# Gate matmuls of a gated recurrence: full-height block-diagonal weights, or pairs of 64-row blocks in the two halves of the array

## The chip, the cores and the metric

The kernel runs on one core of a Trainium2 chip. The metric is device time in microseconds (us) of one launch. Besides the launches that were only timed there is one execution with a hardware profile, and all rows shown come from such profiles. In them PE is the matmul engine (TensorE), PEld its weight loads, DVE is VectorE, ACT is ScalarE, POOL is GpSimd, SP is SyncE, and a q behind a name means that engine's queue of instructions that only issue transfers or wait.

## The reference

One layer of a decoder block, 2048 positions by 1024 features, in float32. One input projection feeds two branches. Branch A is banded, dilated attention. Branch B is a width-4 convolution and a gated linear recurrence (RG-LRU). Both are gated, projected, merged, projected again and normalised. The part that matters here is the two gates of the recurrence, r and i: each is a matmul with a block-diagonal matrix of 16 blocks of 64 by 64.

```python
proj = x @ w_in + b_in
q, k, v, g_attn, u_lru, g_lru, gate_logits = split(proj)
...                                             # branch A: attention
u = causal_depthwise_conv(u_lru, conv_w, conv_b)
xb = u.reshape(B, S, 16, 64)
r = sigmoid(einsum('bsgi,gij->bsgj', xb, w_r).reshape(B, S, C) + b_r)
i = sigmoid(einsum('bsgi,gij->bsgj', xb, w_i).reshape(B, S, C) + b_i)
log_a = -8.0 * r * softplus(-lam)
a, mult = exp(log_a), sqrt(max(-expm1(2.0 * log_a), 0))
h = associative_scan(h[t] = a[t] * h[t-1] + mult[t] * i[t] * u[t])
...
out = (sigmoid(gA) * y_a + sigmoid(gB) * y_b) @ w_out + b_out
return layer_norm(alpha * x + out)
```

## The kernel before

Everything is feature-major: 128 features on the partitions, positions along the free axis in chunks of 512 (`CH`). A float32 product is made of three matmuls in the type fp32r: both factors are split into a rounded high part and a remainder, and high times high, high times low and low times high are added up in one PSUM bank.

The program has three stages. The first is the input projection, from the start to about 1480 us. It is cut into steps (`plan`), each a pair of 128-feature columns for two chunks of positions; a step has seven products (a Strassen-like scheme) of twelve 128x128x512 matmuls. One product is one tick of the loop over `where`. The matmuls of a product all stand on line 598 (`product`), whatever the tiles; their results land in one of four PSUM banks `q` and are taken out by `evacuate`. Around the products runs everything that hangs on the projection's results: rotary embedding, stores, the gates of the branches and the whole recurrence. Each of these is a generator (a chain) that asks at every yield for free slots and for a share of an engine's time (`Ask`); `run_chains` lets it go on in some tick when both are there. The order of each engine's queue is the order in which this Python code emits, and nothing moves it later. The second stage is the attention (about 1480 to 1830 us), the third the output projections and the normalisation.

The recurrence is the chain `lru(i, c, ub)`: 8 groups `i` of 128 features (two 64-blocks each) by 4 chunks `c` of positions, 32 in all, at most two alive at a time. In it, in this order:

- SP fetches the gate weights `gr` (lines 434 and 435): the host has laid out `wr[i]` and `wi[i]` as 128x128 matrices, two 64x64 blocks on the diagonal and zeros beside them. This happens 16 times, twice for each group. ACT (line 452) and DVE split them into high and low, `gw`.
- The convolution's result `v` is split into `vh` and `vl`.
- `gates` hands PE six matmuls, lines 468 to 470, three for r into one PSUM bank `g`, three for i into the other. They are put in by `pe_later`, which means after the sixth matmul of a product of the next tick.
- ACT reads the two banks with a tanh each (lines 481 and 482, into `tr` and `ti`; the sigmoid's half and shift are folded in later), then runs three more operations on `tr`, lines 483 to 485. DVE waits for `ti` on line 486.
- The rest, to the scan on line 503, is DVE and ACT work on 128x512 tiles.

Of the kernel before, what the change touches and what calls it, by code (L numbers as in the profile page):

```python
# [8 lines left out]
F32 = mybir.dt.float32  # L9
F32R = mybir.dt.float32r  # L10
AF = mybir.ActivationFunctionType
ALU = mybir.AluOpType
# [3 lines left out]
P = 128  # L16
# [4 lines left out]
CH = 512  # L21
# [10 lines left out]
def hybrid_block_kernel(ctx: ExitStack, tc: tile.TileContext, a: dict, out: bass.AP):  # L32
    nc = tc.nc
    sp, act, dve, pool, pe = nc.sync, nc.scalar, nc.vector, nc.gpsimd, nc.tensor

    def flat(t):
        return t.bitcast(F32)
# [37 lines left out]
    lr = cst.tile([P, 8, 8], F32, name="lr")  # L75
    act.dma_start(lr, a["lru_vec"])
    brh = cst.tile([P, 2, 8], F32, name="brh")
    sp2 = cst.tile([P, 8], F32, name="sp2")


    X = ctx.enter_context(tc.tile_pool(name="X", bufs=1))
# [11 lines left out]
    def pe_later(lag, fn):  # L93
        pe_late.append((now["n"] + lag, fn))
# [27 lines left out]
    ps = stA.enter_context(tc.tile_pool(name="ps", bufs=2, space=PSUM))  # L122
# [5 lines left out]
    def take(name, dt=F32R):  # L128
        if not vacant:
            raise RuntimeError(f"no slot at {now['n']}: {[x[1].name if hasattr(x[1],'name') else x[1] for x in home.values()]} chains {len(chains)}")  # L130
        i = vacant.pop(0)
        t = sl_p.tile([P, CH], dt, tag=f"s{i}", name=name)
        home[id(t)] = (i, t)
        return t

    def give(*ts):
        for t in ts:
            vacant.append(home.pop(id(t))[0])

    def give_sent(*ts):  # L140

        for t in ts:
            later(2, lambda t=t: give(t))
# [69 lines left out]
    def tt(eng, out, in0, in1, op):  # L213
        eng.tensor_tensor(out=out, in0=in0, in1=in1, op=op)  # L214
# [202 lines left out]
    GLG, GW = {}, {}  # L417
# [5 lines left out]
    def lru(i, c, ub):  # L423
        nm = f"{i}_{c}"
        f = FT_U + i
        if c == 1 and i in put_off:
            yield Ask(lag=0, need=1, keep=1, cond=lambda: len(ub_free) > 1)
            ub = ub_free.pop(0)
            sp.dma_start(ub[:, 3:3 + CH], u_scr[i])
        bring_gw = c in ((0, 1) if i in put_off else (0, 2))  # L430
        if bring_gw:
            yield Ask(lag=0, need=1, keep=1)
            gr = take("gr" + nm, F32)
            sp.dma_start(gr[:, 0:P], a["wr"][i])
            sp.dma_start(gr[:, P:2 * P], a["wi"][i])
        if c == 1 and i in put_off:
            yield Ask(lag=4)
        yield Ask(lag=0, need=1, keep=6, cond=lambda: gate["live"] < 2 and begun[i] == c, ACT=1.3, DVE=2.7)
        gate["live"] += 1
        begun[i] += 1  # L440
        v = take("v" + nm, F32)
        act.activation(ub[:, 0:3], ubs[:, i, c, 0:3], AF.Copy)
        act.activation(v, ub[:, 0:CH], AF.Identity, scale=lrn[:, 0, i:i + 1], bias=lr[:, 4, i:i + 1])
        for j in range(1, 4):
            dve.scalar_tensor_tensor(out=v, in0=ub[:, j:j + CH], scalar=lrn[:, j, i:i + 1], in1=v,
                                     op0=ALU.mult, op1=ALU.add)
        act.activation(ubs[:, i, c + 1, 0:3], ub[:, CH:CH + 3], AF.Copy)
        ub_free.append(ub)
        if bring_gw:
            yield Ask(ACT=.4, DVE=.4, lag=2, need=1, keep=1)  # L450
            w = GW[i] = take("gw" + nm)
            act.activation(w[:, 0:2 * P], gr[:, 0:2 * P], AF.Copy)
            tt(dve, w[:, 2 * P:], gr[:, 0:2 * P], flat(w[:, 0:2 * P]), ALU.subtract)
            give(gr)
        yield Ask(lag=0, cond=lambda: gated[i] == c)
        gw = GW[i].rearrange("p (l j f) -> p l j f", l=2, j=2)
        yield Ask(need=2, keep=1, ACT=.66, DVE=.75)
        vh, vl = take("vh" + nm), take("vl" + nm)
        act.activation(vh, v, AF.Copy)
        tt(dve, vl, v, flat(vh), ALU.subtract)  # L460
        yield Ask(lag=2, cond=lambda: not gate["busy"])
        gate["busy"] = True
        pg = []

        def gates():
            for j in range(2):
                g = ps.tile([P, CH], F32, tag="g", name=f"g{j}{nm}", bufs=2)
                pe.matmul(g, gw[:, 0, j], vh, start=True, stop=False)
                pe.matmul(g, gw[:, 0, j], vl, start=False, stop=False)
                pe.matmul(g, gw[:, 1, j], vh, start=False, stop=True)  # L470
                pg.append(g)
            give(vh, vl)
            if c in ((0, 3) if i in put_off else (1, 3)):
                give(GW[i])

        pe_later(1, gates)
        gated[i] = c + 1
        yield Ask(lag=2, need=3, keep=1, ACT=3.3, DVE=.75)
        gate["busy"] = False
        tr, ti, e = take("tr" + nm, F32), take("ti" + nm, F32), take("e" + nm, F32)  # L480
        act.activation(tr, pg[0], AF.Tanh, scale=0.5, bias=brh[:, 0, i:i + 1])
        act.activation(ti, pg[1], AF.Tanh, scale=0.5, bias=brh[:, 1, i:i + 1])
        act.activation(e, tr, AF.Exp, scale=sp2n[:, i:i + 1], bias=sp2n[:, i:i + 1])
        act.activation(e, e, AF.Identity, scale=0.5, bias=half_t)
        act.activation(tr, tr, AF.Tanh, scale=sp2[:, i:i + 1], bias=sp2[:, i:i + 1])
        dve.scalar_tensor_tensor(out=ti, in0=ti, scalar=1.0, in1=v, op0=ALU.add, op1=ALU.mult)
        give(v)
        yield Ask(need=2, keep=1, ACT=2.0, DVE=2.2)
        s, w = take("sq" + nm, F32), take("nw" + nm, F32)
        act.activation(s, tr, AF.Sqrt)  # L490

        dve.scalar_tensor_tensor(out=w, in0=tr, scalar=1.0, in1=e, op0=ALU.add, op1=ALU.mult)
        dve.scalar_tensor_tensor(out=e, in0=w, scalar=2.0, in1=e, op0=ALU.subtract, op1=ALU.mult)
        dve.scalar_tensor_tensor(out=tr, in0=tr, scalar=2.0, in1=e, op0=ALU.mult, op1=ALU.mult)
        give(w)
        yield Ask(ACT=.66, DVE=1.5)
        act.activation(tr, tr, AF.Identity, bias=one_t)
        dve.scalar_tensor_tensor(out=s, in0=s, scalar=-1.0, in1=e, op0=ALU.mult, op1=ALU.mult)
        tt(dve, s, s, ti, ALU.mult)
        give(e, ti)  # L500
        yield Ask(need=1, keep=1, DVE=1.6, cond=lambda: done[i] == c)
        h = take("h" + nm, F32)
        dve.tensor_tensor_scan(out=h, data0=tr, data1=s, initial=hst[:, i, 0:1], op0=ALU.mult, op1=ALU.add)
        dve.tensor_copy(hst[:, i, 0:1], h[:, CH - 1:CH])
        done[i] = c + 1
        gate["live"] -= 1
        give(tr, s)
        if c == 1 and i in put_off:
            yield Ask(lag=0, need=1, keep=3)
            g = GLG[i, 1] = take("glg" + nm, F32)  # L510
            sp.dma_start(g, hb_scr[i * P:(i + 1) * P, CH:2 * CH])
            yield Ask(lag=2)
        yield Ask(POOL=1.4, cond=lambda: (i, c) in GLG)
        g = GLG.pop((i, c))
        tt(pool, g, g, h, ALU.mult)
        give(h)
        yield Ask()
        sp.dma_start(hb_scr[i * P:(i + 1) * P, c * CH:(c + 1) * CH], g)
        give_sent(g)
# [160 lines left out]
    for s, pl in enumerate(plan):  # L680
        if pl[0] and pl[4] == "ug":
            i = pl[1][1][0] - FT_U
            if i not in put_off:
                continue
            at(base[s] - 12, lambda i=i: start_chain(lru(i, 1, None)))
# [168 lines left out]
    def consts():  # L854
        dve.tensor_scalar(out=bh, in0=b72, scalar1=0.5, scalar2=None, op0=ALU.mult)
        dve.tensor_scalar(out=bn, in0=b72, scalar1=-1.0, scalar2=None, op0=ALU.mult)
        dve.tensor_scalar(out=brh, in0=lr[:, 5:7, :], scalar1=0.5, scalar2=None, op0=ALU.mult)
        dve.tensor_scalar(out=lrn, in0=lr[:, 0:4, :], scalar1=-1.0, scalar2=None, op0=ALU.mult)
        dve.memset(ubs, 0.0)
        dve.memset(hst, 0.0)  # L860
# [20 lines left out]
    at(0, lambda: prep_w(0, 1))  # L881
    at(0, lambda: [one_block("B21", kk) for kk in K4])
    at(0, consts)
    at(1, lambda: prep_w(0, 2))
    at(1, lambda: [one_block("B12", kk) for kk in K4])
# [37 lines left out]
    n = len(where)  # L923
# [137 lines left out]
    for m in range(NB + 4):  # L1061
        u, n = divmod(m, 16)
# [156 lines left out]
    for n in range(32):  # L1219
        c, f = divmod(n, 8)  # L1220
# [211 lines left out]
```

## Time and profile before

| | |
|---|---|
| time, three runs | 2267.12, 2267.64, 2272.91 us; median 2267.64 |
| span of the profiled execution, first to last instruction | 2268.7 us |
| PE busy | 2213.9 us (98%), 11032 matmuls |
| PEld busy | 1868.7 us (82%) |
| DVE, ACT, POOL busy | 1752.4 (77%), 1091.3 (48%), 874.6 us (39%) |
| mean granted TensorE clock | 0.991 |

The page gives the profiled execution's span and no other time of it; the median of the timed runs lies 1.1 us below that span. The busy time of PE counts each matmul to its modelled end, and one matmul begins while the one before is still in flight, so PE's real pace is read from the distance between the starts of neighbouring matmuls and not from the mean duration of a matmul.

### The profile page before, as it was taken

Reading aid. Unit: us, or ns where it says so; the run is one execution under the profiler, and the core shown is the slowest. Engines: PE = TensorE matmul, PEld = TensorE weight load, DVE = VectorE, ACT = ScalarE, POOL = GpSimd, SP = SyncE. Lnnn points to the kernel's source line nnn. Section 1 sums busy time; section 2 is a strip of 40 time slices with the busy share of each in tenths; the row PEclk is TensorE's granted clock in tenths of the full one; section 3 lists DMA queues with packets and bytes.
Section 4 is the critical chain, followed back from the end, with each engine's and each line's share of the span. In section 5 each row is a group of like instructions: output and inputs, shape, how many; then the busy total and the mean of one; then the engine's idle time right before and its main releaser. Section 6 shows DMA issues by size and latency. Waiting matters only on the chain.

```text
span 2268.7 us, 34220 instructions
## 1 busy us (share of the span) xinstructions
PE 2213.9 (98%) x11032; PEld 1868.7 (82%) x11032; DVE 1752.4 (77%) x3234; ACT 1091.3 (48%) x1982; POOL 874.6 (39%) x640
## 2 busy tenths in 40 slices
PE   7999999999999999999999999989999999999998
PEld 6888878888787788888888888878999888788887
DVE  8788878999898877778778878655666668967777
ACT  5344545456455656556566566555666621121010
POOL 1545544555454022222222212257676426722220
PEclk9999999999999999999999999999999999999999
DMA  7998897988987777686888787897786679884441
GB/s 227 268 259 254 244 266 222 273 267 269 273 266 249 258 215 225 201 241 208 252 276 258 249 250 237 251 256 176 206 217 160 191 234 316 287 271 167 130 140 65
DMA packets 327954, 526.01 MB, mean 232 GB/s; under 512 B 97120, under 2 KB 138080, under 8 KB 322912
## 3 DMA queue, kind: packets, MB, share of 16 engines
q1 hardware_dynamic: 297008, 479.05, 68.1%
q0 software_dynamic: 10080, 18.35, 5.1%
q10 hardware_dynamic: 20688, 26.42, 3.7%
q8 instruction: 88, 1.44, 0.3%
q14 instruction: 90, 0.74, 0.1%
HBM read 318.38 MB, written 190.64 MB: 224 GB/s over the span
## 4 chain that ended last, share of the span: by engine, by line
PE 57%; DMA 6%; DVE 2%; ACT 1%; POOL 1%; issue 1%; SPq 1%; ACTq 0%; DVEq 0%; POOLq 0%
PE q L598 29%; PE o L1012 4%; PE s L973 3%; PE z L1304 2%; PE z L1305 2%; PE z L1303 2%; PE yb L1198 2%; PE yb L1200 2%; PE yb L1199 2%; PE pt L988 2%; DMA A<-qh_scr 2%; PE ya L1271 1%; PE ya L1272 1%; PE ya L1270 1%; DMA l<-wl_scr 1%
## 5 line engine op out<-in xcount | busy, mean ns | idle before, releaser
L598 PE MATMUL q<-xT,hS 128*128 128x512 f32 x1680 | 520.9, 391 | 7.2 <-ACT e L621 6.0
L598 PE MATMUL q<-xT,l 128*128 128x512 f32 x1120 | 437.1, 390 | 0.0
L598 PE MATMUL q<-xB,hA 128*128 128x512 f32 x1248 | 389.7, 394 | 10.1 <-ACT xB L202 5.7
L598 PEld LDWEIGHTS q<-xT,hS 128*128 128x128 f32 x1680 | 314.9, 188 | 73.0 <-ACT e L621 6.4
L598 PE MATMUL q<-xB,l 128*128 128x512 f32 x904 | 354.6, 392 | 1.4 <-DMA l<-wl_scr 1.3
L598 PEld LDWEIGHTS q<-xB,hA 128*128 128x128 f32 x1248 | 234.7, 189 | 61.0 <-ACT xB L202 5.7
L598 PEld LDWEIGHTS q<-xT,l 128*128 128x128 f32 x1120 | 210.7, 188 | 44.1
L979 ACT ACTIVATE p<-p,osb 128x256 f32<-128x256 f32 (+1 forms) x384 | 156.2, 454 | 118.4 <-DVE osb L977 117.7
L214 POOL TENSOR_TENSOR S<-S,wA 128x512 f32<-128x512 f32 x35 | 45.7, 1306 | 422.6 <-DVE S L214 251.7
L977 DVE CUSTOM_DVE_ANT_0 p<-s,mask 128x256 f32<-128x256 f32 (+1 forms) x384 | 125.2, 364 | 103.0 <-PE s L973 61.5
L598 PEld LDWEIGHTS q<-xB,l 128*128 128x128 f32 x904 | 171.0, 189 | 38.5 <-DMA l<-wl_scr 2.2
L214 POOL TENSOR_TENSOR sw<-sw,sin 128x512 f32<-128x512 f32 x96 | 161.8, 1691 | 70.3 <-DMA sw<-y 64.6
L259 ACT ACTIVATE hA<-wA 128x512 fp32r<-128x512 f32 x218 | 135.5, 624 | 89.6 <-DMA wA<-in_w_in_dram 52.7
L598 PE MATMUL q<-xB,hS 128*128 128x512 f32 x560 | 174.9, 394 | 3.0 <-DVE v L214 3.0
L598 PE MATMUL q<-xT,hA 128*128 128x512 f32 x560 | 173.1, 390 | 3.1 <-ACT hi L323 1.8
L1012 PE MATMUL o<-V,ptb 128*128 128x65 f32 x1200 | 166.4, 277 | 8.0 <-ACT ptb L993 5.3
L1012 PEld LDWEIGHTS o<-V,ptb 128*128 128x128 f32 x1200 | 153.3, 196 | 19.4 <-ACT ptb L993 16.2
L259 ACT ACTIVATE hS<-S 128x512 fp32r<-128x512 f32 x175 | 109.2, 624 | 97.1 <-DVE S L214 51.3
L214 POOL TENSOR_TENSOR l<-wA,hA 128x512 fp32r<-128x512 f32 x68 | 105.2, 1547 | 80.3 <-ACT hA L259 61.6
L973 PE MATMUL s<-B,A 128*128 128x256 f32 (+1 forms) x384 | 116.8, 326 | 10.0 <-DMA A<-qh_scr 6.4
L598 PEld LDWEIGHTS q<-xT,hA 128*128 128x128 f32 x560 | 104.6, 188 | 26.6 <-issue 3.7
L598 PEld LDWEIGHTS q<-xB,hS 128*128 128x128 f32 x560 | 104.7, 189 | 25.1 <-issue 4.1
(196 smaller groups left out, 4853.0 us busy)
## 6 DMA issues: line engine op xcount, KB each, us to landing
wA<-in_w_in_dram SPq DMA_DIRECT2D x253, 256.0 KB, 5.0
wl_scr<-l SPq DMA_DIRECT2D x105, 512.0 KB, 5.3
l<-wl_scr SPq DMA_DIRECT2D x105, 512.0 KB, 4.7
sw<-y SPq DMA_DIRECT2D x384, 64.0 KB, 3.3
wS<-in_w_in_dram SPq DMA_DIRECT2D x70, 256.0 KB, 4.7
wS<-in_w_in_dram POOLq DMA_DIRECT2D x70, 256.0 KB, 6.6
o_scr<-osb ACTq DMA_DIRECT2D x48, 264.0 KB, 5.9
oc<-o_scr SPq DMA_DIRECT2D x48, 264.0 KB, 5.0
```

The costliest lines, as they stand in the source:

```text
L214: eng.tensor_tensor(out=out, in0=in0, in1=in1, op=op)
L259: act.activation(h, r, AF.Copy)
L598: pe.matmul(bank, w[:, ks], x[:, kk, xx], start=(first and i == 0), stop=(last and i == 11))
L973: pe.matmul(s[:, h, (0 if g == 2 and n else lo):256], q, k, start=(i == 0), stop=(i == 1))
L977: dve.tensor_tensor_reduce(out=p[:, h, lo:256], in0=s[:, h, lo:256], in1=mask[:, lo:256], scale=1.0, scalar=3e38, op0=ALU.add, op1=ALU.min ...
L979: act.activation(p[:, h, lo:256], p[:, h, lo:256], AF.Exp, scale=-1.0, bias=mm)
L988: pe.transpose(pt[:, 2 * h + x, :], p[:, h, x * P:(x + 1) * P], ident)
L1012: pe.matmul(o[:, n % 2, h * 65:h * 65 + 65], ptb[:, 2 * h + x, :], V[:, kb, vo + h * 65:vo + h * 65 + 65], start=(x == lo // P), stop=(x = ...
L1198: pe.matmul(yb, WL[f][:, 0, k], xx[:, 0], start=(k == 0), stop=False)
L1199: pe.matmul(yb, WL[f][:, 0, k], xx[:, 1], start=False, stop=False)
L1200: pe.matmul(yb, WL[f][:, 1, k], xx[:, 0], start=False, stop=(k == 7))
L1303: pe.matmul(z, mh[:, k], w[:, 0, hs], start=(k == 0), stop=False)
```

## The change

The diagonal matrices of 128 rows go. A group's two 64-feature blocks are each kept in their own half of the partitions, as a 64x128 matrix: in the lower half (partitions 0 to 63) block 2i with its r weights in columns 0 to 63 and its i weights in columns 64 to 127; in the upper half block 2i+1 with i first and r second. A gate evaluation is then three pairs of matmuls of 64 rows: in each pair one matmul works on the rows 0 to 63 and writes bank `g0`, the other on the rows 64 to 127 and writes bank `g1`. In the built program these matmuls carry a tile of 64x128, at row 0 and at row 64, where all others have 128x128. The number of matmuls stays at six for each gate evaluation.

Each bank now holds r of one block in one half of its partitions and i of the same block in the other. So the two tanh of 128 partitions become four of 64, and two of them write another half than they read. The biases `brh` are gathered to match by four small transfers on ACT's queue at the start of the program. The weights are fetched by four transfers of 64x64 where two of 128x128 were, and the two operations that split them work on 128x128 where they worked on 128x256.

```diff
+    HALF = (slice(0, 64), slice(64, P))
+    for hs, os in (HALF, HALF[::-1]):
+        act.dma_start(brh[hs, 0], a["lru_vec"][hs, 5])
+        act.dma_start(brh[hs, 1], a["lru_vec"][os, 6])
...
             gr = take("gr" + nm, F32)
-            sp.dma_start(gr[:, 0:P], a["wr"][i])
-            sp.dma_start(gr[:, P:2 * P], a["wi"][i])
+            for hs, n in ((HALF[0], ("wr", "wi")), (HALF[1], ("wi", "wr"))):
+                for j in range(2):
+                    sp.dma_start(gr[hs, HALF[j]], a[n[j]][i, hs, hs])
...
-            act.activation(w[:, 0:2 * P], gr[:, 0:2 * P], AF.Copy)
-            tt(dve, w[:, 2 * P:], gr[:, 0:2 * P], flat(w[:, 0:2 * P]), ALU.subtract)
+            act.activation(w[:, 0:P], gr[:, 0:P], AF.Copy)
+            tt(dve, w[:, P:2 * P], gr[:, 0:P], flat(w[:, 0:P]), ALU.subtract)
...
-        gw = GW[i].rearrange("p (l j f) -> p l j f", l=2, j=2)
+        gw = GW[i].rearrange("p (l f) -> p l f", f=P)
...
         def gates():
-            for j in range(2):
-                g = ps.tile([P, CH], F32, tag="g", name=f"g{j}{nm}", bufs=2)
-                pe.matmul(g, gw[:, 0, j], vh, start=True, stop=False)
-                pe.matmul(g, gw[:, 0, j], vl, start=False, stop=False)
-                pe.matmul(g, gw[:, 1, j], vh, start=False, stop=True)
-                pg.append(g)
+            pg[:] = [ps.tile([P, CH], F32, tag="g", name=f"g{j}{nm}", bufs=2) for j in range(2)]
+            for k, (l, x) in enumerate(((0, vh), (0, vl), (1, vh))):
+                for hs, g in zip(HALF, pg):
+                    pe.matmul(g, gw[hs, l], x[hs], start=(k == 0), stop=(k == 2))
...
-        act.activation(tr, pg[0], AF.Tanh, scale=0.5, bias=brh[:, 0, i:i + 1])
-        act.activation(ti, pg[1], AF.Tanh, scale=0.5, bias=brh[:, 1, i:i + 1])
+        for h, (hs, os) in enumerate((HALF, HALF[::-1])):
+            act.activation(tr[hs], pg[h][hs], AF.Tanh, scale=0.5, bias=brh[hs, 0, i:i + 1])
+            act.activation(ti[hs], pg[h][os], AF.Tanh, scale=0.5, bias=brh[os, 1, i:i + 1])
...
-        dve.tensor_scalar(out=brh, in0=lr[:, 5:7, :], scalar1=0.5, scalar2=None, op0=ALU.mult)
+        dve.tensor_scalar(out=brh, in0=brh, scalar1=0.5, scalar2=None, op0=ALU.mult)
```

On PE, this is the first gate evaluation in the program, group 0 and chunk 0, in the middle of a product `q0` of step 6. `g00` and `g10` are the two banks, `vh0` and `vl0` the parts of the convolved input, `gw0` the weights. Before:

```order
L598 MATMUL q0_6_1450<-xB11_272,l0_6_1349 128x512
L468 MATMUL g00_0_1457<-vh0_0_1379,gw0_0_1352 128x512
L469 MATMUL g00_0_1457<-vl0_0_1380,gw0_0_1352 128x512
L470 MATMUL g00_0_1457<-vh0_0_1379,gw0_0_1352 128x512
L468 MATMUL g10_0_1461<-vh0_0_1379,gw0_0_1352 128x512
L469 MATMUL g10_0_1461<-vl0_0_1380,gw0_0_1352 128x512
L470 MATMUL g10_0_1461<-vh0_0_1379,gw0_0_1352 128x512
L598 MATMUL q0_6_1450<-xB11_272,hA11_6_1347 128x512 x2
```

And the same place in the changed program, whose line numbers are 4 to 6 higher:

```order
L602 MATMUL q0_6_1456<-xB11_276,l0_6_1355 128x512
L474 MATMUL g00_0_1463<-vh0_0_1385,gw0_0_1358 128x512
L474 MATMUL g10_0_1464<-vh0_0_1385,gw0_0_1358 128x512
L474 MATMUL g00_0_1463<-vl0_0_1386,gw0_0_1358 128x512
L474 MATMUL g10_0_1464<-vl0_0_1386,gw0_0_1358 128x512
L474 MATMUL g00_0_1463<-vh0_0_1385,gw0_0_1358 128x512
L474 MATMUL g10_0_1464<-vh0_0_1385,gw0_0_1358 128x512
L602 MATMUL q0_6_1456<-xB11_276,hA11_6_1353 128x512 x2
```

The six stand at the same place between the matmuls of the projection. They now alternate between the two banks, and so between the two halves of the array, where they filled one bank after the other.

On ACT, the same gate evaluation a little later, from the evacuation before it to the three operations on `tr0` behind it. Before:

```order
L259 ACTIVATE hA22_6_1502<-wA22_6_1257 128x512
L481 ACTIVATE tr0_0_1506<-g00_0_1457,brh_198 128x512
L482 ACTIVATE ti0_0_1507<-g10_0_1461,brh_198 128x512
L483 ACTIVATE e0_0_1508<-tr0_0_1506,sp2n_227 128x512
L484 ACTIVATE e0_0_1508<-e0_0_1508,half_t_211 128x512
L485 ACTIVATE tr0_0_1506<-tr0_0_1506,sp2_199 128x512
L259 ACTIVATE hS4_6_1531<-S4_6_1318 128x512
```

After:

```order
L263 ACTIVATE hA22_6_1508<-wA22_6_1263 128x512
L485 ACTIVATE tr0_0_1512<-g00_0_1463,brh_198 64x512
L486 ACTIVATE ti0_0_1513<-g00_0_1463,brh_198 64x512
L485 ACTIVATE tr0_0_1512<-g10_0_1464,brh_198 64x512
L486 ACTIVATE ti0_0_1513<-g10_0_1464,brh_198 64x512
L487 ACTIVATE e0_0_1514<-tr0_0_1512,sp2n_231 128x512
L488 ACTIVATE e0_0_1514<-e0_0_1514,half_t_215 128x512
L489 ACTIVATE tr0_0_1512<-tr0_0_1512,sp2_199 128x512
L263 ACTIVATE hS4_6_1539<-S4_6_1324 128x512
```

Two operations more stand ahead of everything that follows on ACT, and `ti0` is whole only after the fourth. Apart from these places, the two more transfers for each fetch of weights and the four at the start, the order on every engine is as before.

## The prediction

> **What bounds the kernel now.** I read the stages first. The view by windows gives the busy time of each engine in stretches of the projection stage, which ends near 1480 us and holds all 32 gate evaluations. The first column is the stretch and its length; a number after x is a count of instructions.
>
> ```profile
> core 0: us, PE busy (x) PEld busy (x) DVE busy (x) ACT busy (x) POOL busy (x), PEclk, DMA share, GB/s
> 200.00:400.00 200.00, 194.92 (x879) 159.52 (x878) 169.01 (x203) 100.79 (x165) 100.74 (x75) 0.99 0.86 248
> 400.00:600.00 200.00, 199.16 (x878) 164.26 (x877) 185.70 (x216) 101.98 (x170) 110.00 (x81) 1.00 0.90 266
> 600.00:800.00 200.00, 194.31 (x844) 158.77 (x843) 169.51 (x222) 112.88 (x188) 67.84 (x52) 0.99 0.84 265
> 800.00:1000.00 200.00, 200.00 (x907) 165.66 (x906) 153.12 (x210) 111.44 (x181) 45.81 (x31) 1.00 0.74 218
> 1200.00:1481.00 281.00, 279.67 (x1234) 231.25 (x1232) 222.89 (x298) 172.08 (x270) 72.60 (x50) 1.00 0.80 250
> ```
>
> PE is the bound: it is busy all 200 us from 800 to 1000 us. Before 800 us DVE stands close behind (185.70 of 200 us from 400 to 600), after it there is room (153.12). ACT is at most about 61% busy (172.08 of 281 us). So a microsecond taken from PE is a microsecond won in the later part, and perhaps less in the earlier, where PE also waits a few times. A delay on ACT or DVE costs something only where it reaches PE.
>
> Next, the timeline of PE at the first gate evaluation: start, length, line, tiles.
>
> ```profile
> 137.04 0.39 PE L598 MATMUL q<-xB,l 128*128 128x512 f32 x1
> 137.27 0.39 PE L468 MATMUL g<-vh,gw 128*128 128x512 f32 x1
> 137.50 0.39 PE L469 MATMUL g<-vl,gw 128*128 128x512 f32 x1
> 137.72 0.39 PE L470 MATMUL g<-vh,gw 128*128 128x512 f32 x1
> 137.95 0.39 PE L468 MATMUL g<-vh,gw 128*128 128x512 f32 x1
> 138.18 0.39 PE L469 MATMUL g<-vl,gw 128*128 128x512 f32 x1
> 138.40 0.39 PE L470 MATMUL g<-vh,gw 128*128 128x512 f32 x1
> 138.63 0.62 PE L598 MATMUL q<-xB,hA 128*128 128x512 f32 x2
> ```
>
> Each matmul lasts 0.39 us, but one starts every 0.227 us. The six occupy PE from 137.27 to 138.63, 1.36 us, and the projection goes on without a gap on either side. Thirty-two times 1.36 is 43.5 us: all that the gates cost PE now, of which perfect pairing could take half, 21.8 us or 1.0%.
>
> **The change part by part.**
>
> *Pairs.* If the two halves of a pair run side by side, three pairs need 3 x 0.227 = 0.68 us. No row of this trace has a 64-row matmul, so this is bounded: 0.68 us below, and 6 x 0.227 = 1.36 us if the halves go one after the other. I take the low end, because the two work on different rows of the array and write different banks, and nothing that one needs is made by the other.
>
> The weights could still set the pace, since six loads remain for three pairs. The attention's short matmuls show how fast loads can go. Here eight matmuls of 65 columns stand in one row, and the next row begins when they are through:
>
> ```profile
> 1600.60 1.00 PE L1012 MATMUL o<-V,ptb 128*128 128x65 f32 x8
> 1601.41 0.31 PE L973 MATMUL s<-B,A 128*128 128x128 f32 x1
> ```
>
> From 1600.60 to 1601.41 is 0.81 us, 0.10 us for each load with its matmul. Two loads, 0.20 us, fit under the 0.227 us of a pair. Only the second load of the first pair stands alone: 0.10 us more.
>
> *Whether loads may run ahead.* This is the load of the first gate matmul, on PEld:
>
> ```profile
> 137.05 0.19 PEld L468 LDWEIGHTS g<-vh,gw 128*128 128x128 f32 x1
> ```
>
> It lies inside the projection's matmul of 137.04, which uses the same 128 rows. The Trainium skill (TensorE: Matmul & The Clock Gate, Part 3: Packing small matmuls) says that a load overlaps a matmul in flight only where their row groups differ; this trace does not agree. By that rule the second and third pair would each have to wait for their loads, and the sum below would lose about 0.4 us for each gate evaluation. I keep to the row.
>
> *Two switches.* PE goes from 128-row to 64-row tiles and back around every gate evaluation. Nothing in this trace shows such a switch. At the least it costs nothing. The nearest row for the other end is a restart of PE from empty, when a matmul cannot begin until the one before has left the array and its weights come in uncovered:
>
> ```profile
> 313.65 0.39 PE L598 MATMUL q<-xB,l 128*128 128x512 f32 x1
> 315.79 0.70 PE L598 MATMUL q<-xT,hA 128*128 128x512 f32 x2 [1.75 <-ACT hi L323]
> 316.32 0.40 PE L598 MATMUL q<-xT,l 128*128 128x512 f32 x1
> ```
>
> From 313.65 to 315.79 are 2.14 us; without the 1.75 us of waiting 0.39 remain, one whole matmul where the pace is 0.227: 0.16 us lost. The next two take 0.53 us (315.79 to 316.32) instead of 0.45: 0.08 more. A restart so costs 0.24 us, two switches 0.48. I take this end. The Trainium skill (TensorEngine Tiling (Array Packing), Tiling Modes) says that a change of the tiling mode drains the engine, which speaks against the change; it gives no time, and no run so far shows it.
>
> The block then comes to 0.68 + 0.10 + 0.48 = 1.26 us against 1.36. That is 0.10 us for each evaluation, **3.2 us** over 32, and all of it in the stage that PE bounds.
>
> *Two more tanh.* The first row is from the answer on the `g` banks and all that touches them: who waited for their readers, with the total in us and the number of waits. The others are from the timeline at the first gate evaluation.
>
> ```profile
>   DVE ti L486: 7.7, 5
> ...
> 141.20 0.68 ACT L481 ACTIVATE tr<-g,brh 128x512 f32<-128x512 f32 x1
> 141.77 0.69 ACT L482 ACTIVATE ti<-g,brh 128x512 f32<-128x512 f32 x1
> 142.34 0.82 ACT L483 ACTIVATE e<-tr,sp2n 128x512 f32<-128x512 f32 x1
> 143.24 0.68 DVE L486 SCALAR_TENSOR_TENSOR ti<-ti,v 128x512 f32<-128x512 f32 x1
> ```
>
> One tanh follows the other after 0.57 us. A tanh of 64 partitions and 512 columns isn't in the trace; it costs from half that to the whole, and I take the whole, because the columns are as many. ACT then has 2 x 0.57 = 1.14 us more in each evaluation, 36.5 us in all, on an engine that is idle for 38% of the time or more, so it costs nothing by itself. What it moves is `ti`: whole 1.14 us later. Behind the waiting DVE operation are queued the evacuations of the projection's banks, and PE waits for those. Here DVE came to `ti` 0.78 us after the tanh's end (142.46 to 143.24), so 0.36 us of waiting would be new. Over all evaluations the new waiting lies between 0 and 36.5 us; with a place like this one as the middle it is some 12 us of DVE, against 47 idle microseconds in the 200 from 800 us on and 14 in the fullest stretch. Where PE itself waits for evacuations, it is little:
>
> ```profile
> PE q L598 <- DVE v L214: 2.6, 1, 2.6
> PE q L598 <- DVE u L214: 0.7, 2, 0.5
> PE q L598 <- DVE u L214: 1.1, 2, 0.8
> ```
>
> (Total us, times, longest; the first two from the first 500 us, the third from the next 500.) Four banks of `q` give the queue a run of several ticks. I put what reaches PE at **+0.5 us**. If that cover failed and every new wait reached PE it would be the third rival below.
>
> *Weights and biases.* Splitting 128x128 instead of 128x256 makes DVE and ACT faster. The rows are the group of DVE's split (busy us, mean ns, idle before it), SP's issue of one of the two transfers (min, median and max ns), and the timeline of ACT at the start:
>
> ```profile
> L214 DVE TENSOR_TENSOR gw<-gr,gw 128x256 fp32r<-128x256 f32 x16 | 9.0, 561 | 5.5 <-ACT gw L452 5.5
> L434 SPq DMA_DIRECT2D gr<-in_wr_dram x16: 333/436/3583, 93.7 to 1381.9; - x16
> 1.20 0.45 ACTq L76 DMA_DIRECT2D lr<-in_lru_vec_dram  x1
> 1.68 1.28 ACT L259 ACT_TABLE_LOAD   x1 [1.68 <-PEq L1421]
> 4.30 0.63 ACT L259 ACTIVATE hA<-wA 128x512 fp32r<-128x512 f32 x1 [1.34 <-DMA wA<-in_w_in_dram]
> ```
>
> At most 9.0 us of DVE could go; none of it is on PE's path, so it counts as nothing. SP issues two transfers more at a median 0.436 us, 0.87 us each of 16 times; the transfers queued behind them are issued several ticks ahead of use, and this too I take at nothing, up to 14 us if each delay reached PE. The four transfers at the start add 4 x 0.45 = 1.8 us on ACT's queue ahead of the table load. ACT waited 1.34 us for the first weights there, so at most 0.46 us remain: **+0.5 us**, less if the next transfer is what is late.
>
> *Sum.* -3.2 + 0.5 + 0.5 = -2.2 us. The profiled span of 2268.7 would become 2266.5, and the median of 2267.64, which I carry forward, **2265.4 us**, -0.1%.
>
> **The rivals.**
>
> *Cheap switches.* If a switch costs nothing visible, the block is 0.78 us, 0.58 less, 18.6 us over 32: 2267.6 - 18.6 + 1 = 2250. For it: between other kinds of matmuls the pace in the rows above shows no seam. Against it: those all use the whole array. Chance 0.3, prices down to some 0.15 us a switch included.
>
> *Halves one after the other, with drained switches.* Then the block is 1.36 + 0.48 = 1.84 us, 0.48 more, 15.4 us over 32: 2267.6 + 15.4 + 1 = 2284. It decides from a block of 1.57 us on (6.8 us over 32). For it: six loads, six instructions, and a type that this trace shows only on the full array. Against it: separate rows and banks. A milder form has the same place: the halves run together, but the loads of the second and third pair can't run ahead. That adds 2 x 0.20 = 0.40 us to my 1.26, a block of 1.66, 9.6 us over 32 and 2278. The rule of the Trainium skill on loads cited above (TensorE: Matmul & The Clock Gate) leads there; the quoted load speaks against it. Chance 0.2, of which 0.06 for the milder form.
>
> *The late `ti` reaches PE.* If the some 12 us of DVE's new waiting are passed on, the gain of 3.2 turns into 2267.6 - 3.2 + 12 + 0.5 = 2277. It needs DVE to be behind PE at most evaluations; from 400 to 600 us it almost is, after 800 us not. Chance 0.12.
>
> That the change does not do what it says is no rival: the built program has the 64-row tiles.
>
> **How the numbers follow.** A measurement of this kernel tells about 0.3%, 6.8 us, from no change. The forecast has 0.38, of which 0.30 within that bound, 0.05 faster and 0.03 slower. Cheap switches give 0.28 faster and 0.02 the same, serial halves 0.17 slower and 0.03 the same, the late `ti` 0.12 slower. Faster 0.33, same 0.35, slower 0.32. The range takes in the whole of the first two rivals, 2250 to 2284; the likeliest case alone spans 2260 (switches at 0.15) to 2270.
>
> **What would show it.** Per evaluation, the distance on PE from the first gate matmul to the projection's next: 1.26 us if I am right, 0.78 with cheap switches, 1.8 or more with serial halves. The two matmuls of a pair should start within 0.1 us of each other. A seam at each end of about 0.24 us is the switch. DVE's wait at the `ti` operation should rise from 7.7 to some 20 us, and PE's own waits stay near their present sum. I am wrong if the pairs start 0.2 us apart or more, or if PE's new idle time has DVE or ACT as its releaser near the gates.

## The result, and the profile after

The change made the kernel slower: a median of 2276.7 us in ten runs (2269.9 to 2282.3) against 2267.4 us in ten of the kernel before; the ratio is 1.0043, with a 95% interval of 1.0027 to 1.0059. A second series on another occasion gave 2278.0 against 2267.0, ratio 1.0048 (1.0032 to 1.0064). The forecast was 2265.4 us, a little faster.

The profiled execution of the changed kernel is the fastest of its ten (2269.9 us, a span of 2267.8), and the ends of the two profiles are almost the same. So I compare stretches that hold the same work. The projection's matmuls are the same 6072 in both kernels and in the same order, so the trace can be cut at the same two of them: number 1110 (counted from 0), shortly before the fourth gate evaluation, and number 3160, where the second half of the positions begins. The view by windows of the kernel before, middle stretch (9 gate evaluations) and last (20):

```profile
279.92:779.70 499.78, 488.63 (x2147) 400.17 (x2146) 440.22 (x536) 259.30 (x429) 235.38 (x176) 0.99 0.87 261
779.70:1480.20 700.50, 699.15 (x3129) 578.42 (x3128) 545.92 (x748) 418.87 (x678) 160.32 (x109) 1.00 0.78 238
```

The same of the changed kernel (columns: stretch and length, then busy us and instructions of PE, PEld, DVE, ACT, POOL):

```profile
284.08:790.03 505.95, 489.57 (x2147) 394.50 (x2145) 442.38 (x535) 272.24 (x447) 238.67 (x177) 0.99 0.85 257
790.03:1485.70 695.67, 694.08 (x3129) 563.97 (x3128) 542.51 (x748) 446.81 (x719) 159.79 (x109) 1.00 0.78 240
```

Up to the first cut 4.2 us are lost (284.1 against 279.9), in the middle 6.2; the last stretch wins 4.8. In the middle PE's idle time grew from 11.2 to 16.4 us with the same number of matmuls. The view of PE's waits shows whom it waits for there. These are the rows that name DVE (total us, times, longest), before:

```profile
PE q L598 <- DVE v L214: 3.0, 2, 2.6
PE q L598 <- DVE u L214: 1.3, 3, 0.8
PE q L598 <- DVE y L214: 1.2, 1, 1.2
```

and in the changed kernel:

```profile
PE q L602 <- DVE v L218: 3.6, 3, 2.7
PE q L602 <- DVE u L218: 3.0, 4, 1.1
PE q L602 <- DVE y L218: 2.6, 1, 2.6
PE q L602 <- DVE y L548: 1.2, 2, 0.7
```

That is 5.5 us before and 10.4 after. PE's waits for ACT there are 5.6 and 5.9 us. So nearly all of the new idle time waits for DVE.

The timeline of PE at the first gate evaluation, a row for each pair, and below it the next row of the kernel before behind those that the prediction shows:

```profile
139.12 0.39 PE L602 MATMUL q<-xB,l 128*128 128x512 f32 x1
139.44 0.50 PE L474 MATMUL g<-vh,gw 64*128 64x512 f32 x2
139.78 0.40 PE L474 MATMUL g<-vl,gw 64*128 64x512 f32 x2
140.01 0.39 PE L474 MATMUL g<-vh,gw 64*128 64x512 f32 x2
140.34 0.73 PE L602 MATMUL q<-xB,hA 128*128 128x512 f32 x2
140.91 0.39 PE L602 MATMUL q<-xB,l 128*128 128x512 f32 x1
```

```profile
139.08 0.39 PE L598 MATMUL q<-xB,l 128*128 128x512 f32 x1
```

The pairs run together: two matmuls lie in 0.39 to 0.50 us, where one lasts 0.39. The second and third pair are 0.23 us apart. Each change of the tile's height is paid at two steps: on the way in 0.32 us from the projection's matmul to the first pair (139.12 to 139.44) and 0.34 us to the second pair, on the way out 0.33 us (140.01 to 140.34) and then 0.57 us for two matmuls of the projection (140.34 to 140.91), which took 0.45 us before (138.63 to 139.08). Against a pace of 0.227 that is 0.20 to 0.22 us for each change. From the projection's matmul ahead to the third one behind, it is 1.79 us (139.12 to 140.91) against 2.04 before (137.04 to 139.08). So PE wins 0.25 us for each evaluation, 8.0 us over 32. The same stands at nearly all of the others.

The timeline of ACT at that evaluation:

```profile
143.04 0.67 ACT L485 ACTIVATE tr<-g,brh 64x512 f32<-64x512 f32 x1
143.72 0.69 ACT L486 ACTIVATE ti<-g,brh 64x512 f32<-64x512 f32 x1
144.42 0.68 ACT L485 ACTIVATE tr<-g,brh 64x512 f32<-64x512 f32 x1
145.13 0.68 ACT L486 ACTIVATE ti<-g,brh 64x512 f32<-64x512 f32 x1
145.84 0.82 ACT L487 ACTIVATE e<-tr,sp2n 128x512 f32<-128x512 f32 x1
```

A tanh of 64 partitions lasts as long as one of 128, and the next follows 0.70 us later, not 0.57. From the first tanh to the operation behind them are 2.80 us (143.04 to 145.84) where it was 1.14 (141.20 to 142.34): 1.66 us more, not 1.14. DVE's wait at `ti` rose as follows, from 7.7 us in 5 waits:

```profile
  DVE ti L490: 34.0, 23
```

And the start, on ACT's queue:

```profile
1.68 0.53 ACTq L81 DMA_DIRECT2D brh<-in_lru_vec_dram  x1
2.24 0.60 ACTq L82 DMA_DIRECT2D brh<-in_lru_vec_dram  x1
2.87 0.62 ACTq L81 DMA_DIRECT2D brh<-in_lru_vec_dram  x1
4.21 0.49 ACTq L82 DMA_DIRECT2D brh<-in_lru_vec_dram  x1
4.74 1.28 ACT L263 ACT_TABLE_LOAD   x1 [4.74 <-DMA wA<-in_w_in_dram]
```

The four small transfers, with the gap between the third and the fourth, take ACT from 1.68 to 4.70 us, 3.0 us, and the table load stands behind them. PE begins at 7.23 us instead of 5.75.

### The profile page after: what moved, and what is told of

It is laid out like the page before. It is cut to its first block, busy times and chain, and to the rows that moved or that the text cites. A ratio compares the mean times of both kernels' runs of the same rounds, so it can differ in the third digit from the quotient of the medians.

```text
span 2267.8 us, 34369 instructions
## 1 busy us (share of the span) xinstructions
PE 2207.4 (97%) x11032; PEld 1842.5 (81%) x11032; DVE 1754.4 (77%) x3234; ACT 1135.5 (50%) x2046; POOL 878.1 (39%) x640
## 4 chain that ended last, share of the span: by engine, by line
PE 56%; DMA 6%; DVE 4%; ACT 2%; issue 1%; POOL 1%; SPq 1%; ACTq 0%; DVEq 0%; POOLq 0%
PE q L602 29%; PE o L1016 4%; PE s L977 3%; PE z L1308 2%; PE z L1309 2%; PE z L1307 2%; PE yb L1204 2%; PE yb L1202 2%; PE yb L1203 2%; DMA A<-qh_scr 2%; PE pt L992 2%; PE ya L1275 1%; PE ya L1276 1%; PE ya L1274 1%; ACT p L983 1%
## 5 line engine op out<-in xcount | busy, mean ns | idle before, releaser
L1280 POOL TENSOR_TENSOR me<-gA,ybr 128x512 f32<-128x512 f32 x32 | 52.6, 1656 | 182.0 <-DVE gA L1279 157.3
```

The costliest lines, as they stand in the source:

```text
L1280: pool.tensor_tensor(out=ME[c][:, f], in0=ga, in1=yb, op=ALU.add)
```

## Experiments

Three theories first. A: the two more tanh make `ti` late, DVE waits, PE waits for DVE. B: the small transfers cost it. C: the 64-row tiles cost something themselves. The times are medians; all ratios are to the kernel before on the same chip, whose median was 2267.0 to 2267.3 us. The table collects all runs: the ratio's interval, and from the one profile of each the lengths of the three stretches between the same matmuls (3, 9 and 20 gate evaluations). The rest of the program is the same work in all of them, and took 774 to 785 us up to the last matmul of PE. That is a spread as wide as the effects, so one profile of a kernel tells less than its median; and some profiled executions are far from the median of their kernel (changed 7 us below; pairs late 7, start packed 6, packed inputs and fetch by four 5 us above). The rows from "changed, again" to "ti first", from "packed inputs" to "pairs, less ACT" and from "start packed" on were each measured on a chip of their own.

| kernel | time, us | ratio (95%) | to 1110 | 1110 to 3160 | 3160 to the last |
|---|---|---|---|---|---|
| before | 2267.4 | | 279.9 | 499.8 | 700.4 |
| changed | 2276.7 | 1.0043 (1.0027 to 1.0059) | 284.1 | 506.0 | 695.7 |
| changed, again | 2278.0 | 1.0048 (1.0032 to 1.0064) | 284.1 | 505.0 | 701.6 |
| halves only | 2271.2 | 1.0024 (1.0012 to 1.0036) | 277.9 | 504.1 | 702.6 |
| pairs only | 2264.1 | 0.9981 (0.9969 to 0.9994) | 284.4 | 496.8 | 694.8 |
| ti first | 2276.8 | 1.0040 (1.0025 to 1.0055) | 285.3 | 505.6 | 698.3 |
| packed inputs | 2269.0 | 1.0007 (0.9998 to 1.0017) | 279.2 | 510.0 | 698.7 |
| pairs late | 2258.6 | 0.9960 (0.9948 to 0.9973) | 279.9 | 500.3 | 695.1 |
| pairs early | 2273.2 | 1.0031 (1.0019 to 1.0043) | 278.9 | 505.7 | 698.9 |
| pairs, less ACT | 2271.4 | 1.0029 (1.0017 to 1.0041) | 281.3 | 507.1 | 695.8 |
| start packed | 2272.2 | 1.0024 (1.0011 to 1.0036) | 279.5 | 506.7 | 702.3 |
| fetch by four | 2268.2 | 1.0005 (0.9992 to 1.0017) | 280.0 | 498.3 | 700.8 |
| start by four | 2270.2 | 1.0011 (1.0000 to 1.0023) | 281.8 | 500.3 | 699.4 |
| late, new budget | 2269.4 | 1.0006 (0.9995 to 1.0018) | 279.9 | 498.0 | 699.4 |

### The changed kernel again

> The changed kernel once more, beside the others on one chip. Theory A (the two more tanh make ti late, DVE waits for it, PE waits for DVE's evacuations before 780 us, and PE's waits bring stretches at half clock): slower than before by 0.2 to 0.6%, its profile with DVE waits at ti near 34 us and, where the time is long, more half-clock stretches than the earlier profile (mean clock 0.992). Theory B (the small transfers): the same time. Theory C (the 64-row tiles themselves bring the half clock or cost elsewhere): the same time.

2278.0 us. Its profile is near the median of its runs and shows a further loss. The timeline of PE, then the granted clock (the column of 0.50 and 1.00) by windows:

```profile
1328.43 0.64 PE L602 MATMUL q<-xB,hA 128*128 128x512 f32 x2
1332.73 0.64 PE L602 MATMUL q<-xB,l 128*128 128x512 f32 x1 [3.66 <-DMA l<-wl_scr]
1333.16 1.06 PE L602 MATMUL q<-xB,hA 128*128 128x512 f32 x2
```

```profile
1300.00:1328.00 28.00, 27.67 (x123) 21.79 (x122) 22.02 (x30) 10.67 (x21) 8.87 (x6) 1.00 0.81 231
1333.00:1336.00 3.00, 3.00 (x8) 2.35 (x8) 2.97 (x5) 2.73 (x4) 0.00 (x0) 0.50 1.13 452
```

PE waits 3.66 us for a transfer (1.05 us at this place before) and then runs for some 3 us at half the clock, a matmul each 0.43 us. This wait is thus paid with more than its length. That fits the spread of the changed kernel's ten runs, whose mean granted clock goes from 0.992 in the fastest to 0.988 in the slowest; that waits make the whole of the spread was not shown.

### Halves only

```diff
-        act.activation(tr, pg[0], AF.Tanh, scale=0.5, bias=brh[:, 0, i:i + 1])
-        act.activation(ti, pg[1], AF.Tanh, scale=0.5, bias=brh[:, 1, i:i + 1])
+        for hs in (slice(0, 64), slice(64, P)):
+            act.activation(tr[hs], pg[0][hs], AF.Tanh, scale=0.5, bias=brh[hs, 0, i:i + 1])
+            act.activation(ti[hs], pg[1][hs], AF.Tanh, scale=0.5, bias=brh[hs, 1, i:i + 1])
```

> The kernel before, its matmuls, weights and biases untouched, with each of the two gate tanh cut into two of 64 partitions in the order tr, ti, tr, ti. Theory A: slower than before by more than the change was, as PE gains nothing back: 9.3 us measured plus 11.9 us that the pairs gave PE minus 1.8 us of the start = 19 us, 2287 us; DVE's wait at ti rises from 8 to about 34 us. Theory B and theory C: no change, 2267 us, within 3 us.

2271.2 us: the sign is theory A's, the size is not, 4 us and not 19 (or 15, by the 8.0 us for the pairs that the rows above give). It also showed what stretches the block on ACT, in its timeline:

```profile
139.89 0.67 ACT L482 ACTIVATE tr<-g,brh 64x512 f32<-64x512 f32 x1
140.46 0.67 ACT L483 ACTIVATE ti<-g,brh 64x512 f32<-64x512 f32 x1
141.15 0.69 ACT L482 ACTIVATE tr<-g,brh 64x512 f32<-64x512 f32 x1
141.74 0.67 ACT L483 ACTIVATE ti<-g,brh 64x512 f32<-64x512 f32 x1
142.43 0.82 ACT L484 ACTIVATE e<-tr,sp2n 128x512 f32<-128x512 f32 x1
```

Two operations on the same half follow after 0.57 or 0.59 us, as whole ones do; from the lower half to the upper, and from the upper to the whole operation behind, it is 0.69. In the changed kernel every step goes to another half, of the input or of the output, and every step takes 0.70.

### Pairs only

The changed kernel with the two tanh of the kernel before, `tr` from `pg[0]` and `ti` from `pg[1]`.

> The changed kernel with two tanh of 128 partitions as before, one for each bank; r and i of half the blocks are so mixed up and the output is not the reference's, but every engine has the work of the change less the two extra tanh. Theory A: faster than before, by 11.9 us of PE less 1.8 us at the start: about 2257 us. Theory B: as slow as the change, near 2276 us. Theory C: as slow as the change, with a mean clock of 0.988 to 0.991.

2264.1 us: faster than before, so theory C falls. The expectations had counted 0.37 us of gain for an evaluation, 11.9 us in all, and so left out the last step of each return; by the 8.0 us that the rows above give, A stands for some 2261 us. Of the 8.0 us 5.1 are missing, and 4.5 us are lost ahead of matmul 1110 (284.4 against 279.9), where no tanh can have a part. The other two stretches by windows:

```profile
284.40:781.20 496.80, 486.41 (x2147) 393.88 (x2146) 442.44 (x536) 259.10 (x429) 236.26 (x177) 0.99 0.86 262
781.20:1476.10 694.90, 694.25 (x3129) 564.08 (x3128) 542.93 (x748) 417.14 (x678) 159.99 (x110) 1.00 0.78 240
```

The 9 evaluations of the middle stretch gain 3.0 us and the 20 of the last 5.6, about what PE's 0.25 us make (2.3 and 5.0). So what the changed kernel loses in the middle comes with the extra tanh: 9.2 us between these two profiles, 6.0 of them idle time of PE (10.4 to 16.4) and 3.2 busy time for the same matmuls (486.4 to 489.6).

### ti first

```diff
         for h, (hs, os) in enumerate((HALF, HALF[::-1])):
-            act.activation(tr[hs], pg[h][hs], AF.Tanh, scale=0.5, bias=brh[hs, 0, i:i + 1])
             act.activation(ti[hs], pg[h][os], AF.Tanh, scale=0.5, bias=brh[os, 1, i:i + 1])
+        for h, hs in enumerate(HALF):
+            act.activation(tr[hs], pg[h][hs], AF.Tanh, scale=0.5, bias=brh[hs, 0, i:i + 1])
```

> The changed kernel with its four tanh in another order: the two halves of ti first, then the two of tr. ti is whole after two operations as in the kernel before, tr after four. Theory A: DVE's wait at ti falls from 34 us to below 12 us and most of the loss goes: 2257 to 2264 us. If it is ACT's longer work as such that delays PE (theory A2: everything behind the tanh on ACT comes 1.14 us later): near 2276 us. Theory B and theory C: near 2276 us.

DVE's wait at `ti` did fall:

```profile
  DVE ti L491: 12.2, 8
```

The time did not: 2276.8 us, and 505.6 us in the middle stretch. Theory A as I had put it falls. DVE's waits at `ti` are a place where the delay shows, not its cause: with `ti` early they turn up behind other operations of ACT. In the middle stretch DVE waits for ACT 34 us in the kernel before, 42 in the changed one and still 41 here, and PE's waits for DVE stay too (10.4 and 10.8 us). What is left is A2: the longer block delays all that stands behind it on ACT, and DVE gets one or the other of it late.

### Packed inputs

The host lays out the pair weights as one 128x128 matrix for each group, and the i biases with the halves exchanged; one transfer brings the weights, and `brh` is made from `lr` as before.

> The changed kernel with the pair weights and the biases laid out by the host, so that one transfer of 128x128 brings the weights and none of the four small ones stands at the start. Theory A2 (the block of tanh on ACT is 1.66 us longer, and what is behind it on ACT comes later; where DVE is nearly full, PE waits): only the start of 1.5 us comes back, about 2275 us. Theory B (the transfers cost it): about 2257 us, before less the 11.9 us of the pairs.

2269.0 us: 9 us less than the changed kernel's second series, six times what A2 gave the transfers. B holds for this part. In the profile the gain is in the first stretch, 279.2 us against 284.1; the middle stretch, with 510.0 us, is the longest of all, so nothing of the loss there came back with the transfers.

### Pairs late, pairs early

Inputs as in the last run, and a flag chooses matmuls, weights and tanh of each evaluation; `early` has the opposite condition.

```diff
+        pair = c >= 2 or (c == 1 and i in put_off)
```

> Inputs as in the run before; pairs and halves only for the 20 gate evaluations of the second half of the projection stage, the first 12 as in the kernel before. Theory A2: DVE has room there, so most of 20 x 0.37 us = 7.4 us is gained: 2260 to 2264 us. Theory D (every evaluation with halves costs the same wherever it stands, 10 us over 32): 2267 + 20/32 x 10 = 2273 us.

> The opposite: pairs and halves for the first 12 gate evaluations, the last 20 as in the kernel before. Theory A2: the whole loss sits here, at least 8 us: 2275 us or more. Theory D: 2267 + 12/32 x 10 = 2271 us.

2258.6 us for the pairs in the last 20 evaluations, 2273.2 for those in the first 12. Theory D falls: the same exchange gains 8.5 us in one half and loses 6 in the other. The early run by itself lies between its two expectations. The late one gains more than the 5.0 us that PE can gain in 20 evaluations; where the rest comes from is open. By windows, with the pairs late:

```profile
279.90:780.20 500.30, 489.94 (x2148) 401.07 (x2147) 441.75 (x538) 260.59 (x431) 238.06 (x177) 0.99 0.86 261
780.20:1475.30 695.10, 694.27 (x3128) 564.11 (x3127) 536.95 (x746) 444.99 (x716) 161.63 (x110) 1.00 0.77 239
```

With the pairs early:

```profile
278.90:784.60 505.70, 488.39 (x2148) 393.33 (x2147) 441.53 (x535) 272.02 (x446) 238.46 (x176) 0.99 0.84 257
784.60:1483.50 698.90, 698.90 (x3129) 578.41 (x3128) 542.91 (x748) 419.33 (x678) 159.53 (x109) 1.00 0.77 239
```

In the middle stretch DVE is busy for 88 and 87%, and pairs with halves take 5 us more there than whole tanh; in the last it is busy for 77 and 78%, and the pairs win 3.8 to 5.3 us although ACT has the same extra work. All profiles together bear out the middle: 496.8 to 500.3 us in the six with whole tanh there, 504.1 to 510.0 in the eight with halves. The last stretch is less clear: pairs with halves take 695.1 to 702.3 us there, the four kernels with neither 698.9 to 700.8.

The waits tell the two stretches apart. With halves DVE waits longer for ACT in both: 38 to 43 us against 31 to 35 in the middle, 59 to 71 against 48 to 50 in the last. But PE's waits for DVE grow in the middle alone, from 3.8 to 5.5 us with whole tanh to 7.4 to 11.1 with halves; in the last stretch they are nil in all profiles but one (0.2 us). PE's few waits there are for transfers, nearly all of them.

The version with late pairs is the fastest kernel of this study, 0.4% under the one before.

### Pairs, less ACT

The changed kernel without the operations `e = 0.5 e + 0.5` and `tr = tr + 1` on ACT.

> The changed kernel without the two later identity operations of each gate evaluation on ACT (the half and shift of e, and the plus one of tr), so the output is not the reference's. ACT has then 1.4 us less in each evaluation, about what the halves added. Theory A2 in the form that ACT's total work is what delays: near the run with pairs only, 2264 us. If it is the half-height operations themselves (writing the other half of the partitions, reading a bank twice): as the change, 2277 us.

2271.4 us, between the two. The first stretch is shorter than the changed kernel's (281.3 against 284.1), the last as long as in its shorter profile, the middle no shorter (507.1 us). Only one of the two operations stands in the burst right behind the tanh, so ACT's total work is not what counts in the middle; that the place of the delay does is an argument, not shown.

### The transfers apart

Start packed: the changed kernel without the four at the start. Fetch by four and start by four: the kernel before with one of the two additions.

> The changed kernel with the biases laid out by the host, so without the four small transfers at the start, but with the four transfers of 64x64 for each fetch of weights. All transfers together were worth 9 us (2278.0 against 2269.0). If the fetches carry it (theory B1, SP's queue): 2276 us, only the start's 1.5 to 1.8 us back. If the start carries it (theory B2, a shift of the start that costs more than itself): about 2270 us.

> The kernel before with each fetch of gate weights as four transfers of 64x128 in place of two of 128x128, nothing else. Theory B1: slower than before by 3 to 7 us, 2270 to 2274 us, with DVE waiting for a weight transfer near 277 us of the profile. Theory B2: 2267 us.

> The kernel before with the biases brought by four small transfers on ACT's queue at the start, nothing else. Theory B1: 1.5 to 1.8 us slower, 2269 us. Theory B2: 5 us or more slower, 2272 us.

2272.2, 2268.2 and 2270.2 us. The start seems the greater part: 4.5 to 5.8 us in the changed kernel (2276.7 or 2278.0 to 2272.2), 3 us in the kernel before, where the interval begins at nothing and 1.5 us can be seen directly. The fetches by four are worth some 3 us in the changed kernel (2272.2 to 2269.0, two chips) and can't be told from nothing in the kernel before. Neither B1 nor B2 has it whole, and each of these differences is hardly larger than its uncertainty. At one place the cost of the fetch by four can be seen. SP's queue in the run with pairs only:

```profile
267.31 3.15 SPq L440 DMA_DIRECT2D gr<-in_wr_dram  x1
270.51 1.23 SPq L440 DMA_DIRECT2D gr<-in_wi_dram  x2
271.78 0.59 SPq L440 DMA_DIRECT2D gr<-in_wr_dram  x1
272.48 1.00 SPq L225 DMA_DIRECT2D wA<-in_w_in_dram  x2
```

DVE and PE, from the same run:

```profile
277.54 0.69 DVE L218 TENSOR_TENSOR S<-S,wA 128x512 f32<-128x512 f32 x1 [3.24 <-DMA wA<-in_w_in_dram]
```

```profile
278.98 0.70 PE L601 MATMUL q<-xB,hS 128*128 128x512 f32 x2 [1.73 <-DVE v L218]
```

The fetch by four holds the weights `wA` behind it on SP's queue, DVE waits 3.24 us for them, and PE 1.73 us for DVE. In the run with packed inputs neither wait is there. The wait needs neither the pairs nor the start: in the run with the fetch by four alone DVE waits 2.79 us at this place and PE 1.2, as B1 had it, and with the start packed PE waits 1.1.

### Late pairs with a new budget

```diff
-        yield Ask(lag=2, need=3, keep=1, ACT=3.3, DVE=.75)
+        yield Ask(lag=2, need=3, keep=1, ACT=5.0 if pair else 3.3, DVE=.75)
```

> The run with pairs in the second half only (2258.6 us), with the planner told that the tanh of a pair evaluation cost ACT 5.0 us and not 3.3, so that what follows is emitted a little later. If ACT's late work still costs something there: 2 to 4 us faster, 2255 us. If ACT has room there as it is: the same, 2258 to 2260 us.

2269.4 us, 11 us worse than without it. Neither expectation holds. The truer price moved operations in much of the second half's order, and the gain went: the last stretch took 699.4 us, and the rest of the program 783. Why is open; it shows that the 8.5 us of the late pairs hang on the order of emission too.

## Why the prediction was wrong

The third rival, the late `ti` that reaches PE, had 2277 us and a chance of 0.12; it has the time, but only half the mechanism, and its sum came out by luck: its -3.2, +12 and +0.5 us were -8.0, about +10 to +14 and +5 to +9. Step by step:

- *PE bounds the stage, and a microsecond taken from it counts, less in the earlier part.* Right: pairs without extra tanh gain 3.0 us in the middle stretch and 5.6 in the last, where PE's 0.25 us for each evaluation make 2.3 and 5.0.
- *Pairs run together, loads run ahead.* Right between pairs: the second pair's loads begin at 139.55 us, inside the pair in flight on the same rows (139.44 to 139.94), and the third pair follows the second after 0.23 us. Across a change they don't run ahead: the first pair's loads begin with its matmuls, at 139.44. The rule of the Trainium skill on loads (TensorE: Matmul & The Clock Gate, Part 3: Packing small matmuls) is again not what the trace shows between pairs.
- *Two switches at 0.24 us and 0.10 us for a load, 3.2 us gained.* The neighbour was well chosen: a change costs 0.20 to 0.22 us, half of it one step later, as behind a restart. The load of 0.10 us on top is not there beside them, so the term was 0.58 us and measured 0.42 to 0.43: PE's gain is 8.0 us, two and a half times the forecast. That there is a seam agrees with the Trainium skill (TensorEngine Tiling (Array Packing), Tiling Modes), which has a change of mode drain the engine; the size is the trace's.
- *Two more tanh: 1.14 us, and +0.5 us of it reaches PE.* This step failed, and it set the sign. The block grew by 1.66 us, DVE's waiting at `ti` by 26.3 us (7.7 to 34.0) where 12 were forecast, and the extra tanh cost 13.9 us with the pairs in place (2264.1 to 2278.0), or 9.9 beside packed inputs (2269.0, by 2267.1 - 8.0 + 9.9). I had counted new waiting at the one DVE operation that reads `ti`, and set it against DVE's idle time over long windows. The run with `ti` first showed that the waiting goes elsewhere when that place is relieved, and the late and early runs that it costs in the earlier part, where DVE is 88% busy. My own windows had shown that stretch. I had named new idle time of PE with DVE as its releaser as a sign of being wrong: 5.5 us became 10.4 in the middle stretch.
- *Without the pairs the same halves cost 4 us.* The prediction had no term for this. That a faster PE is less cover is my reading, not shown. The block in that run is also a little shorter (2.54 us, 139.89 to 142.43 of its timeline). How much of the other 6 to 10 us each of these makes was not separated.
- *The start: 0.46 us at most.* Failed. I took 0.45 us for an issue and let ACT's wait of 1.34 us absorb the rest; the four took 3.0 us together, PE began 1.5 us later, and the run without them is 4.5 to 5.8 us faster than the changed kernel. How 1.5 us become more is open.
- *SP's two more transfers: nothing.* Failed at one place, by 1.7 us of PE's time there and some 3 us in all, within the noise. The order of the program had shown the loads that stand behind them.

The sum in these terms: -8.0 for the pairs, +9.9 to +13.9 for the halves, +9.0 (2278.0 to 2269.0) to +5.1 (2264.1, by 2267.0 - 8.0 + 5.1) for the transfers, the larger of one with the smaller of the other. That makes +10.9 to +11.0, as measured in the second series, but only because halves and transfers are read from the same differences; it proves no more than that two ways of taking them apart differ by 4 us, and each interval is 2 to 4 us wide on either side.

## What to carry to other kernels

Where an engine is not the bound, ask in which stretch its neighbour is: 1.7 us of ACT work cost about a microsecond for each evaluation where DVE was 87 to 89% busy, and 0 to 0.4 us by profile where it was 77 to 78%. That it is DVE's load that makes the difference fits the waits; other things differ between the two stretches too (the DMA engines' share is 0.83 to 0.87 against 0.77 to 0.78), and they were not separated. A gain that depends on such a stretch can be had by changing only the other ones, if the order of emission holds: one order of the late pairs gained 8.5 us, another none. Operations of half the partitions cost ACT as much as whole ones, so a layout that fills the matmul array better can lose more at the eviction. And a few tiny transfers ahead of the first useful instruction delay everything behind them: 3.0 us of issues made PE begin 1.5 us later.

## What the runs showed of the hardware

- Two 64-row matmuls in the two halves of the array run together in the time of one, and so do their loads, as this row of PEld shows (changed kernel, the first pair's two loads; one alone takes 0.19):

```profile
139.44 0.19 PEld L474 LDWEIGHTS g<-vh,gw 64*128 64x128 f32 x2 [0.35 <-issue]
```

- Changing between 128-row and 64-row tiles costs 0.20 to 0.22 us of PE's time each way, about half of it at the change and half one step behind (1.79 us from 139.12 to 140.91, where three pairs and three projection matmuls at 0.227 would take 1.36).
- A tanh of 64 partitions and 512 columns lasts as long on ACT as one of 128 (0.67 to 0.69 us).
- In these rows ACT operations at 512 columns overlap by about 0.1 us where both read and write the same half, or both the whole (0.57 to 0.59 us from start to start), and not where input or output goes from one half to the other (0.68 to 0.71).
- A wait of 3.66 us on PE was followed by about 3 us at half the clock.
